# Forty of 256 tokens leave the dense expert products of a two-layer trunk, their experts' rows gathered by index

## The chip, the cores and the metric

One core of one Trainium2 chip. The metric is the device time of one execution in microseconds (us). Before the change the median of three runs is 1989.61 us (1987.29 to 1992.58). A difference of less than about 0.3% can't be told from none.

## What is computed

A trunk of two layers on T = 256 tokens of D = 1024. Layer 0 mixes tokens by a short convolution and forgetting attention, layer 1 by sparse attention (compressed, selected and window branches). After its mixer each layer has a PEER channel mixer: 8 heads choose 16 of 16384 experts of a single neuron each, by product keys (128 x 128), and sum them with softmax gates.

```python
h = modulate(rms_norm(x, norm_g), shift, scale)
q = (h @ w_q)                       # 8 heads, two halves of 64
s1, s2 = q1 @ keys1.T, q2 @ keys2.T # 128 scores each
# top 16 of each half, top 16 of the 16 x 16 sums, softmax over those 16
act = gelu(sum_d u[idx, d] * h[d])  # per token, head and chosen expert
out = sum(gate * act * v[idx])      # over 8 x 16 experts
x = x + gate_ada * out
```

Shifts, scales and gates (6 x 1024 values a layer) come from `silu(c) @ ada_w`. All is float32.

## The kernel before, in words

**Dense PEER.** The kernel doesn't look experts up. `peer(l, early, late, after)` (L689) multiplies all tokens by all 16384 rows of u, applies gelu, multiplies by a matrix that holds the gate where an expert was chosen and zero elsewhere, and multiplies by all rows of v. The 128 x 128 experts are 128 tiles of 128; the result of the u product stands in two buffers `S` of 64 tiles x 256 tokens.

**Split weights.** Every weight tile of 512 KB is loaded on SP's queue into one of five `raw` buffers (L76) and split into two parts: `hi` by an ACT copy (L82) and `lo` by a DVE subtraction (L83), three buffers each. A product of 1024 terms is then 8 slices x 3 fp32r matmuls (hi·hi, hi·lo, lo·hi; L100), each of 128 x 128 weights by 256 token columns into PSUM.

**Stages of a PEER layer.** `norm` makes h in 8 chunks of 128 features; `score` (one for each of four pairs of heads) projects with w_q and multiplies by the keys; `choose` finds the top 16 on DVE with MAX, MATCH_REPLACE and MAX_INDEX, cut into pieces that the loop below calls one by one; `weigh` makes the gates and brings them and the indices to the layout of the experts (PE transposes). `mm1(j)` is the u product of tiles j and j+1: 48 matmuls, then gelu. The first 32 calls run beside the pieces of `choose`; the second 32 each with two calls of `gating`. `gating(j)` makes, for four tokens, two one-hot matrices (L855, `is_equal`), multiplies one by the gates' high and low halves (L859, on DVE, result `w`), and contracts them by eight f16 matmuls into `pG`, which DVE multiplies into the S tiles that exist (L869) and ACT copies into those that don't yet (L871). `mm2(j)` is the v product: it splits two tiles of S (L885 on ACT, L886 on DVE) and accumulates 48 matmuls in four PSUM banks `yb`. 64 calls in all; then the residual.

**Other work in between.** `ada` (L147 to L150) loads 512 KB and reduces it on DVE (L149). The 48 of layer 1 and 8 of layer 0 are spread over peer(0): 20 in the first half of the u product, the rest in the v product. `exps` (L110) preloads the table with Ln and Exp on ACT; it stands between the u and the v product.

**What sets the order.** The tile scheduler orders instructions on each engine by its own simulation of the program, except where `keep_in_program_order` pins one. An engine takes its instructions strictly in that order.

Of the kernel before, what the change touches and what calls it, by code (L numbers as in the profile page):

```python
# [31 lines left out]
GSCALE = 2.0 ** 15  # L32

# [18 lines left out]
def trunk(ctx: ExitStack, tc: tile.TileContext, xT, c, ada_w, ada_b, norm_g, even_w, even_wf, even_bf,  # L52
          even_cw, qk_g, even_wo, odd_w, odd_wg, odd_bg, odd_g, cmp_pos, cmp_w1, cmp_w2, odd_wo,
          rel_table, buckets, w_q, keys, peer_u, peer_v, out):
# [80 lines left out]
    V.tensor_scalar(rowm, ident[:, 0:1], -31.0, None, op0=ALU.is_le)  # L135
    V.tensor_scalar(ident, ident, 0.0, None, op0=ALU.is_equal)
# [3 lines left out]
    G.iota(lane, pattern=[[1, P]], base=0, channel_multiplier=0, allow_small_or_imprecise_dtypes=True)  # L140
    mean_d = cp.tile([P, 1], F32, name="mean_d")
# [376 lines left out]
    def odd_mixer(l, w1, pos, tn, og, wg, bg, w2, mean_h):  # L518
        with tc.tile_pool(name="odd", bufs=1, reuse_waits="tile") as mp:
# [161 lines left out]
            attend(0, 3)  # L681
            for j in range(4):
                out_proj(l, odd_wo, cat, 0, j, sq)
                attend(1, j)
            for n in range(4):
                out_proj(l, odd_wo, cat, 1, n, sq)


    def peer(l, early, late, after=None):  # L689
# [3 lines left out]
        S = [s0.tile([P, 64, T], F32, name="S0"), pp.tile([P, 64, T], F32, name="S1")]  # L693
        if True:
            h = norm(l, 1, hi, lo, S[0][:, :KC], S[1][:, :KC],
                     [pp.tile([P, T], F32, tag=f"g{n}", bufs=2, name=f"h_t{n}") for n in range(2)], PEER)

# [27 lines left out]
            def parts():  # L725

                if hot[0] is None:
                    hot[0] = cp.tile([P, 4, 1024], F16, tag="x", name="hot")
                x = hot[0]
                return ([x[:, n, :512].rearrange("p (t i) -> p t i", t=4) for n in range(2)],  # L730
                        [x[:, n, 512:].rearrange("p (t j) -> p t j", t=4) for n in range(2)],
                        [x[:, 2 + n // 2, 512 * (n % 2):512 * (n % 2) + 512].rearrange("p (t u) -> p t u", u=2)
                         for n in range(4)])
# [28 lines left out]
            def choose(hp):  # L762
# [27 lines left out]
                for n in range(2):  # L790
# [9 lines left out]
                    yield  # L800

            def weigh():
# [6 lines left out]
                V.tensor_tensor(g, g, z[:, :, :, None].to_broadcast([P, 2, 8, 16]), op=ALU.mult)  # L809
                it, jt, g_hi, g_lo = parts()[2]  # L810
# [6 lines left out]
                gr = pp.tile([P, T], F32, tag="g1", bufs=2, name="gr")  # L817
                V.tensor_scalar(gr, pT[:, :T], GSCALE, None, op0=ALU.mult)
                V.tensor_copy(g_hi, gr[:, :, None].to_broadcast([P, T, 2]))
                V.tensor_tensor(g_lo, gr[:, :, None].to_broadcast([P, T, 2]), g_hi, op=ALU.subtract)  # L820
# [4 lines left out]
            def mm1(j):  # L825
# [3 lines left out]
                for s in range(2):  # L829
                    contract(p[:, s * T:(s + 1) * T], over_d(weights(peer_u[l, j + s]), h))  # L830
                p = p.rearrange("p (a t) -> p a t", a=2)
                s = S[j // 64][:, j % 64:j % 64 + 2]
                n = gated[0]
                if n < T:
# [5 lines left out]
            def gating(j):  # L840
# [3 lines left out]
                sl = slice(4 * b, 4 * b + 4)  # L844
# [6 lines left out]
                def words(v):  # L851
                    return v[:, sl, None].to_broadcast([P, 4, 64, 2])
# [23 lines left out]
            def mm2(j):  # L876
# [3 lines left out]
                vx = []  # L880
                for n in range(2):
                    s = S[j // 64][:, j % 64 + n]
                    v = weights(peer_v[l, j + n])
                    x = Op(None, h.hi[:, (j + n) % KC], h.lo[:, (j + n) % KC])
                    A.activation(x.hi, s, AF.Copy)  # L885
                    V.tensor_tensor(x.lo, s, x.hi.bitcast(F32), op=ALU.subtract)  # L886
                    vx.append((v, x))
                order = [(n, k) for n in range(2) for k in range(KC)]
                for n, k in order if j < 126 else sorted(order, key=lambda o: o[1]):
                    v, x = vx[n]  # L890
                    contract(yb[k // 2][:, (k % 2) * T:(k % 2 + 1) * T],
# [12 lines left out]
            side = pieces()  # L904
# [9 lines left out]
            start = 24  # L914
            lots = spread(early[:20], (64 - start) // 2)
            for j in range(0, 64, 2):
# [3 lines left out]
                if j >= start:  # L920
                    for f in lots[(j - start) // 2]:
                        f()
            for _ in side:
                pass
            for b in range(32):
                for _ in range(2):
                    gating(64 + 2 * b)
                mm1(64 + 2 * b)
            exps()
            for b, fs in enumerate(spread(early[20:], 32)):  # L930
                mm2(2 * b)
                for f in fs:
                    f()
            s0.release()
            got = None
            for b, fs in enumerate(spread(late, 32)):
                mm2(64 + 2 * b)
                if b == 4:
                    cur[0] = x_tile()
                    nc.sync.dma_start(cur[0], xd)  # L940
                if b == 8 and after is not None:
                    got = after()
                for f in fs:
                    f()
            for k in range(KC):
# [3 lines left out]
                else:  # L949
                    power(k, S[1][:, k])  # L950
# [9 lines left out]
    def finish(l):  # L960
        ada_done(l, 0, 6)
        gain(l, 0)
        gain(l, 1)
# [6 lines left out]
    def after():  # L970
# [3 lines left out]
    got = peer(0, adas(0, 5 * KC, 6 * KC) + [gate2] + adas(1, 0, 30),  # L974
               adas(1, 30, 6 * KC) + [lambda: finish(1)], after)
    odd_mixer(1, *got)
    oc[0].release()
    peer(1, [], [])
# [6 lines left out]
def _arrays(i):  # L985
# [52 lines left out]
    a["peer_u"] = i["peer_u"].reshape(L, P, P, KC, P).transpose(0, 2, 4, 3, 1).reshape(L, P, P, D)  # L1038
    a["peer_v"] = i["peer_v"].reshape(L, P, P, D).transpose(0, 2, 1, 3)
# [35 lines left out]
```

## Time and profile before

| | |
|---|---|
| median of the runs | 1989.61 us |
| the profiled execution's own time | 1991.12 us |
| its span in the profile | 1989.3 us |
| mean granted TensorE clock | 0.986 of full |
| PE, DVE, ACT busy | 97%, 74%, 47% of the span |
| bytes read from HBM | 369.16 MB |

The profile is of one execution, taken on the chip. PE is TensorE's matmul, PEld its weight load, DVE VectorE, ACT ScalarE, POOL GpSimd, SP SyncE (its queue issues the loads). A row of a group has line, engine, operation, out<-in with shapes and the count, then the busy time and the mean length of one in ns, then the engine's idle time just before these and what ended it. Matmuls overlap one another, so the length of one record is more than the distance from start to start.

### The profile page before, as it was taken

Reading aid. Unit: us, or ns where it says so; the run is one execution under the profiler, and the core shown is the slowest. Engines: PE = TensorE matmul, PEld = TensorE weight load, DVE = VectorE, ACT = ScalarE, POOL = GpSimd, SP = SyncE. Lnnn points to the kernel's source line nnn. Section 1 sums busy time; section 2 is a strip of 40 time slices with the busy share of each in tenths; the row PEclk is TensorE's granted clock in tenths of the full one; section 3 lists DMA queues with packets and bytes.
Section 4 is the critical chain, followed back from the end, with each engine's and each line's share of the span. In section 5 each row is a group of like instructions: output and inputs, shape, how many; then the busy total and the mean of one; then the engine's idle time right before and its main releaser. Section 6 shows DMA issues by size and latency. Waiting matters only on the chain.

```text
span 1989.3 us, 39878 instructions
## 1 busy us (share of the span) xinstructions
PE 1930.3 (97%) x15994; PEld 1859.0 (93%) x15994; DVE 1468.0 (74%) x3424; ACT 939.3 (47%) x1547; POOL 3.6 (0%) x13
## 2 busy tenths in 40 slices
PE   4899999999999999999999989999999999999999
PEld 3788999999999999999987679999999999999999
DVE  7676999789997666666656859975899975555554
ACT  3445444444444444444456654454444444444443
POOL 0000000000000000000000000000000000000000
PEclk8999999999999999999999999999999999999999
DMA  8866567855455777877743135555554555555554
GB/s 309 262 215 193 177 202 258 273 162 159 150 159 191 233 236 249 294 244 238 228 129 99 41 115 165 177 187 178 159 159 156 154 176 183 181 183 186 183 181 127
DMA packets 105621, 375.44 MB, mean 189 GB/s; under 512 B 12715, under 2 KB 16860, under 8 KB 104540
## 3 DMA queue, kind: packets, MB, share of 16 engines
q1 hardware_dynamic: 104860, 372.38, 58.0%
q8 instruction: 125, 2.05, 0.4%
q10 hardware_dynamic: 576, 0.52, 0.1%
q14 instruction: 60, 0.49, 0.1%
HBM read 369.16 MB, written 6.31 MB: 189 GB/s over the span
## 4 chain that ended last, share of the span: by engine, by line
PE 53%; issue 41%; DMA 3%; DVE 2%; ACT 1%; DVEq 0%; POOL 0%; POOLq 0%; ACTq 0%; SPq 0%
PE pmm L100 19%; PE y L100 19%; PE po L100 2%; DMA raw<-in_ada_w_dram 2%; PE pG L100 1%; PE pq L100 1%; PE pcc L100 1%; PE pwq L100 1%; PE s L638 1%; PE pv L100 1%; DMA S<-in_keys_dram 1%; PE pt L342 1%; PE po_att L653 1%; DMA raw<-in_even_w_dram 1%; PE pb L100 1%
## 5 line engine op out<-in xcount | busy, mean ns | idle before, releaser
L82 ACT ACTIVATE hi<-raw 128x1024 fp32r<-128x1024 f32 x588 | 622.1, 1059 | 899.2 <-PE pmm L100 416.3
L83 DVE TENSOR_TENSOR lo<-raw,hi 128x1024 fp32r<-128x1024 f32 x588 | 717.5, 1221 | 332.2 <-ACT hi L82 331.0
L100 PE MATMUL y<-h_hi,hi 128*128 128x256 f32 x2048 | 579.7, 284 | 6.6 <-ACT h_hi L885 6.6
L100 PE MATMUL pmm<-h_hi,hi 128*128 128x256 f32 x2048 | 584.6, 286 | 0.0
L100 PE MATMUL pmm<-h_hi,lo 128*128 128x256 f32 x2048 | 581.9, 285 | 0.7 <-DVE lo L83 0.7
L100 PE MATMUL pmm<-h_lo,hi 128*128 128x256 f32 x2048 | 582.1, 284 | 0.0
L100 PE MATMUL y<-h_lo,hi 128*128 128x256 f32 x2048 | 580.7, 284 | 0.0
L100 PE MATMUL y<-h_hi,lo 128*128 128x256 f32 x2048 | 578.9, 284 | 0.0
L100 PEld LDWEIGHTS y<-h_hi,hi 128*128 128x128 f32 x2048 | 394.4, 193 | 7.0 <-ACT h_hi L885 7.0
L100 PEld LDWEIGHTS y<-h_lo,hi 128*128 128x128 f32 x2048 | 395.2, 193 | 0.0
L100 PEld LDWEIGHTS y<-h_hi,lo 128*128 128x128 f32 x2048 | 394.0, 193 | 0.0
L100 PEld LDWEIGHTS pmm<-h_hi,lo 128*128 128x128 f32 x2048 | 391.8, 192 | 1.4 <-DVE lo L83 0.9
L100 PEld LDWEIGHTS pmm<-h_lo,hi 128*128 128x128 f32 x2048 | 392.5, 192 | 0.5
L100 PEld LDWEIGHTS pmm<-h_hi,hi 128*128 128x128 f32 x2048 | 392.5, 192 | 0.0
L149 DVE CUSTOM_DVE_ANT_0 raw<-raw,silu 128x1024 f32<-128x1024 f32 x96 | 117.2, 1223 | 93.3 <-DMA raw<-in_ada_w_dram 93.0
L859 DVE TENSOR_TENSOR w<-hot 128x512 f16<-128x512 f16 x256 | 102.8, 418 | 12.4 <-PE pG L100 12.2
L886 DVE TENSOR_TENSOR h_lo<-S,h_hi 128x256 fp32r<-128x256 f32 x256 | 106.0, 418 | 3.2 <-ACT h_hi L885 3.2
L855 DVE TENSOR_TENSOR hot<-hot,lane 128x512 f16<-128x512 f16 x256 | 104.9, 417 | 0.0
L885 ACT ACTIVATE h_hi<-S 128x256 fp32r<-128x256 f32 x256 | 101.6, 402 | 5.5 <-PE y L100 5.5
L100 PE MATMUL pG<-w,hot 128*128 128x128 f16 x1024 | 84.6, 221 | 0.0
L869 DVE TENSOR_TENSOR S<-S,pG 128x256 f32<-128x256 f32 (+5 forms) x252 | 80.1, 347 | 5.0 <-PE pG L100 4.9
L100 PEld LDWEIGHTS <-hot 128*128 128x128 f16 x1024 | 59.2, 98 | 6.8
(269 smaller groups left out, 1845.3 us busy)
## 6 DMA issues: line engine op xcount, KB each, us to landing
raw<-in_peer_u_dram SPq DMA_DIRECT2D x256, 512.0 KB, 3.6
raw<-in_peer_v_dram SPq DMA_DIRECT2D x256, 512.0 KB, 4.2
raw<-in_ada_w_dram SPq DMA_DIRECT2D x96, 512.0 KB, 4.5
raw<-in_even_w_dram SPq DMA_DIRECT2D x24, 512.0 KB, 4.6
raw<-in_odd_w_dram SPq DMA_DIRECT2D x20, 512.0 KB, 4.3
raw<-in_w_q_dram SPq DMA_DIRECT2D x16, 512.0 KB, 4.2
raw<-in_even_wo_dram SPq DMA_DIRECT2D x8, 512.0 KB, 3.5
raw<-in_odd_wo_dram SPq DMA_DIRECT2D x8, 512.0 KB, 3.5
```

The lines of the kernel that those rows point to most:

```text
L82: A.activation(hi, raw, AF.Copy)
L83: V.tensor_tensor(lo, raw, hi.bitcast(F32), op=ALU.subtract)
L100: PE.matmul(dst, a, b, start=start and n == 0, stop=stop and n == len(pairs) - 1, **kw)
L149: V.tensor_tensor_reduce(out=w, in0=w, in1=silu, op0=ALU.mult, op1=ALU.add, scale=1.0, scalar=0.0, accum_out=mods[:, l, m:m + 1])
L342: PE.transpose(pt[:, n * P:(n + 1) * P], p[:, n * P:(n + 1) * P], ident)
L638: PE.matmul(s[half][:, x:x + n + pad], qT[r, ch, t * P:(t + 1) * P], k[r, gp, :n + pad], start=True, stop=True)
L653: PE.matmul(po[r, :T], vt[:, 0, cs[half]], pt[half][:, :T], start=(b == 0), stop=False)
L855: V.tensor_tensor(pairs(x), words(v), pairs(lane[:, None].to_broadcast([P, 4, P])), op=ALU.is_equal)
L859: V.tensor_tensor(pairs(x), pairs(o), words(g), op=ALU.mult)
L869: V.tensor_tensor(s[:, :n], s[:, :n], p[:, 64 * f:64 * f + n], op=ALU.mult)
L885: A.activation(x.hi, s, AF.Copy)
L886: V.tensor_tensor(x.lo, s, x.hi.bitcast(F32), op=ALU.subtract)
```

## The change

Forty tokens (columns 0 to 39; `NS = 40`) leave the dense products. All matmuls of the u and the v product then have 216 columns instead of 256 (`TD`), and there are 54 gatings a layer instead of 64.

- `by_token` copies h of the forty tokens three times side by side (120 columns), transposes it with eight fp32 matmuls into two PSUM banks `pht` and copies it to `ht`: 120 partitions, each with one token's 1024 features. It stands ahead of `score(0)`.
- `indices` and `gates3` make the experts' numbers and gates for the forty tokens, 44 columns on 120 partitions: 128 experts a token are dealt to three partitions. Two of the three thirds are moved to their partitions by DMAs from ACT's queue.
- `dots` and `values`: 44 indirect DMAs on POOL's queue each fetch 120 rows of 4 KB of u (a second copy of it, laid out by row, is a new input), and 44 reductions on DVE multiply them by `ht`; then gelu, times the gates; then 44 more fetch rows of v, and 44 operations on DVE sum them. They use three `gat` buffers. `folded` adds the three thirds of a token into `yb` with eight fp32 matmuls near the end of the v product.
- The multiplication of the one-hot matrix by the gates goes from DVE (one operation for four tokens) to ACT (one for each token, the gate as scale).
- `mm2` splits both tiles of S with one operation on each engine.
- `exps` is called at the end of `dots`.
- Of layer 1's 48 adas 16 stay in peer(0), 24 go to the odd mixer (`meanwhile`: one with each weight tile), 8 to peer(1).

```diff
+NS = 40
+TD = T - NS
+NP = 3 * NS
+NU = 44
...
+            later = [lambda m=m: ada(l, m) for m in range(2 * KC, 5 * KC)]
+            def ahead():
+                if later:
+                    later.pop(0)()
+            meanwhile[0] = ahead
...
-        S = [s0.tile([P, 64, T], F32, name="S0"), pp.tile([P, 64, T], F32, name="S1")]
+        S = [s0.tile([P, 64, TD], F32, name="S0"), pp.tile([P, 64, TD], F32, name="S1")]
...
+            hd = h.at(lambda a: a[:, :, NS:])
+            def by_token():
+                x = pp.tile([P, D], F32, tag="gat", bufs=3, name="gat")[:, :KC * NP].rearrange("p (k g t) -> p k g t", k=KC, g=3)
+                V.tensor_copy(x, h.raw[:, :, None, :NS].to_broadcast([P, KC, 3, NS]))
+                for n in range(2):
+                    p = bank("a", "pht")
+                    for k in range(4):
+                        PE.matmul(p[:NP, k * P:(k + 1) * P], x[:, 4 * n + k].rearrange("p g t -> p (g t)"), ident,
+                                  start=True, stop=True)
+                    A.activation(ht[:NP, n * 512:(n + 1) * 512], p[:NP], AF.Copy)
...
+            def thirds(dst, src, n, w):
+                V.tensor_copy(dst[:NS, n:n + w], src(0))
+                for g in (1, 2):
+                    A.dma_start(dst[g * NS:(g + 1) * NS, n:n + w], src(g))
...
+            def gather(table, u):
+                x = pp.tile([P, D], F32, tag="gat", bufs=3, name="gat")
+                G.indirect_dma_start(out=x[:NP], out_offset=None, in_=table,
+                                     in_offset=bass.IndirectOffsetOnAxis(ap=idx[:NP, u:u + 1], axis=0))
+                return x
+            def dots():
+                got = {}
+                for u in range(NU + 2):
+                    if u < NU:
+                        got[u] = gather(peer_un, u)
+                    if u >= 2:
+                        x = got.pop(u - 2)
+                        V.tensor_tensor_reduce(out=x[:NP], in0=x[:NP], in1=ht[:NP], op0=ALU.mult, op1=ALU.add, scale=1.0,
+                                               scalar=0.0, accum_out=dot[:NP, u - 2:u - 1])
+                    yield
+                A.activation(wt[:NP], dot[:NP], AF.Gelu_apprx_tanh)
+                V.tensor_tensor(wt[:NP], wt[:NP], ga[:NP], op=ALU.mult)
+                exps()
...
+                        x, c = got.pop(u - 2)[:NP], wt[:NP, u - 2:u - 1]
...
+                            V.scalar_tensor_tensor(acc[:NP], x, c, acc[:NP], op0=ALU.mult, op1=ALU.add)
...
-                    contract(p[:, s * T:(s + 1) * T], over_d(weights(peer_u[l, j + s]), h))
+                    contract(p[:, s * TD:(s + 1) * TD], over_d(weights(peer_u[l, j + s]), hd))
...
-                    V.tensor_tensor(pairs(x), pairs(o), words(g), op=ALU.mult)
+                    for t in range(4):
+                        A.activation(x[:, t], o[:, t], AF.Copy, scale=g[:, st][:, t:t + 1])
...
-            side = pieces()
+            side, near, far = pieces(), dots(), values()
+            by_token()
             score(0)
...
-            exps()
-            for b, fs in enumerate(spread(early[20:], 32)):
+            steps = [near] * 27 + [far] * 47
+            turns = spread(steps, 60)
```

Three places show what this does to the order of the instructions. DVE in the first half of layer 0's u product, before (L740 to L786 are `choose`, L83 the split):

```order
L741 MATCH_REPLACE S_1602<-S_1602,psc_1862 128x128
L743 MAX_INDEX S_1602<-S_1602,psc_1862 128x8
L740 MAX S_1602<-psc_1862 128x8
L783 TENSOR_SCALAR S_1602<-S_1602 128x64
L784 TENSOR_SCALAR S_1602<-S_1602 128x64
L83 TENSOR_TENSOR lo<-raw,hi 128x1024
```

The same place now (L780 is the reduction of `dots`, L87 the split):

```order
L780 ISA gat,dot<-gat,ht 120x1024
L780 ISA dot 120x1
L855 MAX_INDEX S_1609<-S_1609 128x8
L852 MATCH_REPLACE S_1609<-S_1609,psc_1893 128x128
L854 MAX_INDEX S_1609<-S_1609,psc_1893 128x8
L851 MAX S_1609<-psc_1893 128x8
L780 ISA gat,dot<-gat,ht 120x1024
L780 ISA dot 120x1
L87 TENSOR_TENSOR lo<-raw,hi 128x1024
```

In the program 18 steps of `dots` are called in the second half of the u product and the rest in the v product; in the order 33 of layer 0's 44 reductions stand ahead of the first one-hot, between the pieces of `choose` and the splits, and so do 34 of layer 1's. All 44 operations of `values` stand beside the gatings.

ACT among the gatings of layer 0, before (L835 and L837 are gelu, L82 the split):

```order
L871 ACTIVATE S_1602<-pG 128x62x4 x2
L82 ACTIVATE hi<-raw 128x1024
L835 ACTIVATE S_1602<-pmm_4465 128x2x240
L837 ACTIVATE pmm_4465<-pmm_4465 128x2x16
L871 ACTIVATE S_1602<-pG 128x60x4
```

And now (L974 is the gate multiply, L783 the gelu of `dots`, L114 the preload of `exps`, L986 the copy from `pG`):

```order
L986 ACTIVATE S_1609<-pG 128x60x4
L949 ACTIVATE S_1609<-pmm_4584 128x2x196
L86 ACTIVATE hi<-raw 128x1024
L783 ACTIVATE wt<-dot 120x44
L114 ACT_TABLE_LOAD
L986 ACTIVATE S_1609<-pG 128x60x4
L86 ACTIVATE hi<-raw 128x1024
L951 ACT_TABLE_LOAD
L951 ACTIVATE pmm_4584<-pmm_4584 128x2x20
L974 ACTIVATE w_4762<-hot 128x128 x4
L974 ACTIVATE w_4767<-hot 128x128 x4
```

Eight activations of 128x128 are added for each gating. The preload of Ln and Exp stands among the gelus, which load their own table again behind it.

ACT at the norm ahead of the odd mixer, before (L177 is Ln, L178 Exp, on the power `pm` of the chunk sums):

```order
L170 ACTIVATE S_1602<-x_sb 128x256 x3
L177 ACTIVATE h_t_11838<-pm,eps 128x256
L178 ACTIVATE h_t_11838<-h_t_11838 128x256
L207 ACTIVATE h_hi<-h_sq,mods,gs 128x256 x2
L193 ACTIVATE h_raw<-h_raw,mods,gs 128x256 x2
```

And now (L188 is Ln, L189 Exp):

```order
L181 ACTIVATE S_1609<-x_sb 128x256 x4
L188 ACT_TABLE_LOAD
L188 ACTIVATE h_t_12096<-pm,eps 128x256
L189 ACT_TABLE_LOAD
L189 ACTIVATE h_t_12096<-h_t_12096 128x256
L218 ACTIVATE h_hi<-h_sq,mods,gs 128x256 x2
```

Each Ln and each Exp in the odd mixer and the norm behind it has a table load of its own ahead of it; there are 30 table loads in the program, 11 before.

## Rows read from the trace of the kernel before

**Rows 1.** The page: span, and busy time of each engine.

```profile
span 1989.3 us, 39878 instructions
PE 1930.3 (97%) x15994; PEld 1859.0 (93%) x15994; DVE 1468.0 (74%) x3424; ACT 939.3 (47%) x1547; POOL 3.6 (0%) x13
```

**Rows 2.** Windows: length, PE, PEld, DVE, ACT, POOL busy, granted clock, DMA share, GB/s.

```profile
210.00:400.00 190.00, 189.30 (x1568) 188.08 (x1568) 173.32 (x545) 86.84 (x100) 0.00 (x0) 1.00 0.71 229
400.00:616.00 216.00, 216.00 (x2031) 212.76 (x2030) 200.84 (x467) 99.52 (x189) 0.00 (x0) 1.00 0.50 158
646.00:985.00 339.00, 339.00 (x2828) 339.00 (x2827) 221.89 (x314) 159.97 (x232) 0.00 (x0) 1.00 0.75 247
1000.00:1200.00 200.00, 190.45 (x1388) 153.76 (x1388) 131.97 (x480) 114.34 (x274) 1.51 (x5) 0.98 0.32 99
1202.00:1390.00 188.00, 188.00 (x1559) 186.98 (x1558) 153.18 (x507) 86.59 (x99) 0.00 (x0) 1.00 0.56 180
1390.00:1607.00 217.00, 217.00 (x2038) 213.76 (x2037) 200.55 (x465) 99.52 (x189) 0.00 (x0) 1.00 0.50 156
1636.00:1960.00 324.00, 324.00 (x2702) 324.00 (x2701) 175.27 (x226) 153.65 (x225) 0.00 (x0) 1.00 0.58 183
```

**Rows 3.** Timeline of PE, second u half: start, length, operation.

```profile
1500.00 0.28 PE L100 MATMUL pmm<-h_lo,hi 128*128 128x256 f32 x1
1500.12 0.28 PE L100 MATMUL pmm<-h_hi,lo 128*128 128x256 f32 x1
...
1502.04 0.68 PE L100 MATMUL pG<-w,hot 128*128 128x128 f16 x9
```

**Rows 4.** Timeline of PE, odd mixer: matmuls of 512 columns.

```profile
1057.21 0.39 PE L100 MATMUL pv<-lo,h_hi 128*128 128x512 f32 x1
1057.44 0.40 PE L100 MATMUL pv<-hi,h_lo 128*128 128x512 f32 x1
```

**Rows 5.** Weight loads: the group of the v product; a timeline row of plain fp32.

```profile
L100 PEld LDWEIGHTS y<-h_hi,hi 128*128 128x128 f32 x2048 | 394.4, 193 | 7.0 <-ACT h_hi L885 7.0
...
61.90 1.20 PEld L296 LDWEIGHTS pf<-wf,h_raw 128*128 128x128 f32 x10
```

**Rows 6.** Groups of instructions on DVE: busy us, mean ns, idle before.

```profile
L83 DVE TENSOR_TENSOR lo<-raw,hi 128x1024 fp32r<-128x1024 f32 x588 | 717.5, 1221 | 332.2 <-ACT hi L82 331.0
L149 DVE CUSTOM_DVE_ANT_0 raw<-raw,silu 128x1024 f32<-128x1024 f32 x96 | 117.2, 1223 | 93.3 <-DMA raw<-in_ada_w_dram 93.0
L859 DVE TENSOR_TENSOR w<-hot 128x512 f16<-128x512 f16 x256 | 102.8, 418 | 12.4 <-PE pG L100 12.2
```

**Rows 7.** Timeline of DVE in a gating of layer 0.

```profile
501.04 0.42 DVE L859 TENSOR_TENSOR w<-hot 128x512 f16<-128x512 f16 x1
501.37 0.59 DVE L869 TENSOR_TENSOR S<-S,pG 128x256 f32<-128x256 f32 x2
```

**Rows 8.** Groups of instructions on ACT.

```profile
L337 ACT ACTIVATE p<-p,sums 128x128 f32<-128x128 f32 x8 | 2.7, 390 | 0.2 <-DVE sums L444 0.2
L110 ACT ACT_TABLE_LOAD x3 | 3.8, 1283 | 0.1
```

**Rows 9.** Timeline of ACT in a gating of layer 0.

```profile
501.81 1.06 ACT L82 ACTIVATE hi<-raw 128x1024 fp32r<-128x1024 f32 x1 [2.22 <-PE pmm L100]
502.77 0.46 ACT L871 ACTIVATE S<-pG 128x144 f32<-128x144 f32 x2
```

**Rows 10.** Timeline of PE at the head of layer 0's PEER.

```profile
183.14 0.58 PE L100 MATMUL pwq<-h_hi,hi 128*128 128x256 f32 x1 [3.61 <-ACT h_hi L207]
...
189.10 0.38 PE L100 MATMUL pwq<-h_hi,hi 128*128 128x256 f32 x1
```

**Rows 11.** DMA issues: operation and count, KB each, us to landing.

```profile
raw<-in_peer_u_dram SPq DMA_DIRECT2D x256, 512.0 KB, 3.6
X<-Xt ACTq DMA_DIRECT2D x2, 128.0 KB, 4.1
```

**Rows 12.** Timeline of PE at the same norm: plain fp32 matmuls.

```profile
177.29 1.02 PE L171 MATMUL pm<-h_sq,mean_d 128*128 128x256 f32 x4
```

More of the change, by code (lines that the diff above doesn't have):

```diff
@@ L684, in odd_mixer @@
                 attend(1, j)
+            meanwhile[0] = None
+            for f in later:
+                f()
+            ada_done(l, 3, 5)
+            gain(l, 1)
             for n in range(4):
@@ new lines, in peer, with values @@
+            sums = [None]
+            def values():
+                got = {}
+                acc = sums[0] = pp.tile([P, D], F32, tag="long", name="acc")
+                for u in range(NU + 2):
+                    if u < NU:
+                        got[u] = gather(peer_v.rearrange("l j i d -> (l j i) d"), u)
+                    if u >= 2:
+                        x, c = got.pop(u - 2)[:NP], wt[:NP, u - 2:u - 1]
+                        if u == 2:
+                            V.tensor_scalar(acc[:NP], x, c, None, op0=ALU.mult)
+                        else:
+                            V.scalar_tensor_tensor(acc[:NP], x, c, acc[:NP], op0=ALU.mult, op1=ALU.add)
+                    yield
@@ L698, in peer, with folded @@
+            def folded():
+                for k in range(KC):
+                    PE.matmul(yb[k // 2][:, (k % 2) * T:(k % 2) * T + NS], sums[0][:NP, k * P:(k + 1) * P], fold[:NP],
+                              start=False, stop=False, skip_group_check=True)
             spare = S[1][:, 32:].rearrange("p a t -> p (a t)")
@@ L919, in peer @@
                     next(side, None)
-                if j >= start:
-                    for f in lots[(j - start) // 2]:
-                        f()
             for _ in side:
                 pass
-            for b in range(32):
-                for _ in range(2):
+            for b, n in enumerate(spread(range(TD // 4), 32)):
+                for _ in n:
                     gating(64 + 2 * b)
                 mm1(64 + 2 * b)
-            exps()
-            for b, fs in enumerate(spread(early[20:], 32)):
+                if b >= 12:
+                    next(near, None)
+            steps = [near] * 27 + [far] * 47
+            turns = spread(steps, 60)
+            lots = spread(early, 28) + [[]] * 4 + spread(late, 32)
+            got = None
+            for b in range(64):
                 mm2(2 * b)
-                for f in fs:
+                for f in lots[b]:
                     f()
[L934 to L938, printed above, removed]
+                for f in turns[b] if b < 60 else ():
+                    next(f, None)
+                if b == 31:
+                    s0.release()
+                if b == 36:
                     cur[0] = x_tile()
                     nc.sync.dma_start(cur[0], xd)
-                if b == 8 and after is not None:
+                if b == 40 and after is not None:
                     got = after()
-                for f in fs:
-                    f()
+                if b == 61:
+                    folded()
             for k in range(KC):
```

89 lines of the change are left out of this document (58 added, 31 removed).

## The prediction

> **What bounds the kernel now.** I read the page first: PE is busy 97% of 1989.3 us, DVE 74%, ACT 47%, and POOL has 13 instructions in all [rows 1]. That is an average over stages with different limits, so I cut the run into stages [rows 2]: first half of the u product (210 to 400 and 1202 to 1390), second half with the gatings (400 to 616 and 1390 to 1607), v product (646 to 985 and 1636 to 1960), odd mixer (1000 to 1200). The reader is to see that PE is full in each PEER stage at a granted clock of 1.00, but that DVE stands at 173 of 190 and 201 of 216 us in the two u halves, at only 222 of 339 in the v product, and that ACT stands near half throughout. So PE sets the time, with little room on DVE in the u halves and much in the v product. The pace of PE itself: two neighbouring fp32r matmuls of 256 columns start 0.12 us apart [rows 3], and the v product of layer 1 gives the same, 324 us / 2702 = 119.9 ns [rows 2].
>
> **What a matmul of 216 columns costs.** The change narrows 12288 of them (2 layers x 2 products x 3072). Two things can set 0.120. If columns do: 512 columns start 0.23 apart [rows 4], so a column costs (230 - 120) / 256 = 0.43 ns and 40 fewer give 120 - 17 = 102.5 ns. If the weight load does: ten plain fp32 loads feeding 8-column matmuls take 1.20 us, and one fp32r load is recorded as 0.193 long [rows 5], so loads follow each other every (1.20 - 0.19) / 9 = 0.112 us even with hardly a column behind them. The fp32r load handles the same 128 columns of 4 bytes and has the same recorded length, so I take **112 ns**: a gain of 8 ns. The ends are 102.5 (load hidden) and 120 (the load already sets the pace).
>
> **The v product.** PE bounds it and DVE and ACT have room [rows 2]: -3072 x 8 = -24.6 us a layer, **-49**. The ends: 0 and 3072 x 2 x 17.5 = -107. The split of S as one operation per pair only shortens idle engines; the reductions moved in and out of it sit on DVE, which has 117 us to spare. The eight folding matmuls are under 3 us and count as nothing. DMA: u and v moved 247 GB/s at a share of 0.75 in 646 to 985 without holding PE [rows 2], which is the level that the first u half reaches when gathers join it.
>
> **First u half.** PE falls to 1536 x 0.112 = 172 us, but the scheduler has put the dots here: 33 in layer 0 and 34 in layer 1 stand before the first one-hot of the gatings, between the pieces of the choice, and DVE is taken in order. A dot is an ada's reduction with 120 for 128 rows, 1.22 us [rows 6]. Layer 0: 173.3 - 20 adas x 1.22 + 33 x 1.22 + 3 for the small index operations = 192.2. Layer 1: 153.2 + 34 x 1.22 + 3 = 197.7. DVE becomes the bound. PE's work before was 1536 x 0.120 = 184.3 in 190 us, so a stage runs 3% over its bound; I charge DVE the same: 198 and 204, that is **+8 and +16**. The gain of PE in this stage is gone.
>
> **Second u half.** ACT takes over the gate multiply. Before, one DVE operation 128x512 of 0.42 us [rows 6], whose neighbours overlap by 0.08 [rows 7], so 0.336; now four activations 128x128 with a scale per partition. The nearest row has that shape and that scale and takes 0.390 [rows 8]; neighbours on ACT overlap by 0.095 (1.06 long, the next after 0.96) [rows 9], so 0.295 each. 54 gatings x 8 x 0.295 = 127.4 us. ACT: 99.5 + 127.4 - 5 (narrower gelus and copies) + two table loads of 1.283 [rows 8] = 224.5 of a stage of 216. DVE: 200.8 - 128 x 0.336 - a sixth of the one-hots and S products (about 13) + 11 dots + 44 values x 1.2 (the split's 1.221 [rows 6] less the overlap, plus a scalar read) = 211. PE: 172 + 432 x 0.0565 [rows 3] = 196. So **ACT** bounds, where it was half idle. Before, PE had 184.3 + 512 x 0.0565 = 213 in 216, 1.3% over; ACT at 227.5 gives **+12 and +11**. The bounds: 0.195 for an activation (nothing but PE's time, gain 20) and 0.39 without overlap (+53).
>
> **Head of PEER.** The eight transposes (16 PE instructions) of by_token stand between the norm's last matmul and the first matmul of the projection. They need every chunk of h. Before, the projection's first 24 matmuls trickled from 183.14 to 189.10 behind the chunks [rows 10] and then ran at 0.12. Now PE waits until the last chunk (189), the copy and the transposes: about 193. What was done by then, 24 + 3.9 / 0.12 = 56 matmuls, is late: 56 x 0.12 = 7 us a layer, **+14**. The ends are 0 and 10 a layer.
>
> **Odd mixer.** The preload of the Ln/Exp table now follows the Gelu of the dots, in the middle of the gatings, where the next gelu loads its own table again; so the mixer and the norm after it load tables 18 times more, 18 x 1.283 = 23 us of ACT, and 22 adas x 1.22 = 27 us of DVE come into a stage of 200 us where ACT has 114 and DVE 132 [rows 2]. Hidden wholly it costs the two Exp loads directly on the chain of the norm, 3 us; wholly exposed 50. PE idles there only 10 of 200 us, so most is covered: **+12**.
>
> **Waits for gathers.** Each of eight pairs of heads now has index work and two DMAs on ACT's queue (a 128 KB one there lands in 4.1 us [rows 11]) before its first gather, and a dot whose rows are late holds the splits queued behind it on DVE, for which PE waits. With three buffers I take 1 us for each: **+8**.
>
> Sum: -49 + 8 + 16 + 12 + 11 + 14 + 12 + 8 = +32. The profiled execution took 1991.1 us, 1.5 above the median of the runs; the forecast is 1991.1 + 32 - 1.5 = **2022**.
>
> **Rivals.** (A) Columns set the pace: 102.5 ns. The u halves stay with DVE and ACT, the v products give -107 for -49: 1964. For it: 128 columns of f16 at 0.0565 [rows 3] and 512 at 0.23 lie near a line through 256. Against it: the 0.112 of bare loads. The Trainium skill (TensorE: Matmul & The Clock Gate, Back-to-back issue gap) has a column rule: an isolated matmul is N / 2.4 + 2.5 ns, which gives 92.5 for 216, and all 12288 at 27.5 less would be -338, or -169 with the v products alone; by that rule 256 columns would take 109, and the trace has 120. Chance 0.18. (B) The covers hold: no slip over the bounds (+2, +10, +8.5, +7.5), 3 for the mixer, 6 for the heads, nothing for gathers: -49 + 37 = -12, 1978. Chance 0.18. (C), slower: gathers bound. All 88 of a layer lie in the two u halves, 426 us by my sum, so from 4.8 us each they set the time; a dot waits for its rows with the splits behind it. At 5.3 us it is 40 us a layer, 2102; at 6 us 102 a layer, 2226. For it: 120 rows of 4 KB, three buffers, indices late; POOL did nothing of this before. Against it: a load of 512 KB lands in 3.6 us [rows 11]. The Trainium skill (DMA: Bandwidth & Descriptors, Anatomy of one DMA) puts a transfer issued by GpSimd at 2 us plus bytes / 436 GB/s, an estimate of 3.1 us for 480 KB; no run here shows a gather. Chance 0.14. (D) fp32r under 256 columns runs at the pace of plain fp32: four of 256 columns take 1.02 us, 0.16 of it the drain of the last (0.28 - 0.12), so 0.215 [rows 3, 12], 0.18 for 216: +12288 x 0.06 = 737, some 2760. Nothing in the trace has fp32r at such a width. Chance 0.05. That the columns are not narrowed is excluded: the order has 128x216 in both products.
>
> **How the numbers follow.** My sum 0.45, A 0.18, B 0.18, C 0.14, D 0.05. A measurement tells 0.3%, 6 us, from no change. A and half of B are faster, and a little of the sum's own spread: 0.28. The rest of B and the sum's lower edge are the same: 0.11. Slower 0.61. The range goes from 1950 (A with good covers) to 2095 (the open ends of the mixer, of ACT's activations or of slow gathers); it leaves out D, most of C and the far end of A. The sum's own range is 1990 to 2060.
>
> **What would show it.** Right: neighbouring 216-column matmuls in the v product 0.112 apart and that stage near 315 and 300 us; DVE at 95% or more in the first u half, with PE's waits there on lo; ACT at 95% or more with the gatings, w ended by ACT; some 30 table loads; the first projection matmul 10 us later after the norm. Wrong: a pitch of 0.103 or 0.120; dots that wait for gat (C); ACT's activations far from 0.295; a mixer that is not longer.

## The result, and the profile after

The changed kernel takes **2172.51 us** (median of four runs, 2162.43 to 2178.16), 1.0912 times the kernel before (95% interval 1.0868 to 1.0955). The forecast was 2022 in a range of 1950 to 2095: slower as forecast, by 182 us where 32 were forecast.

Page of the changed kernel: span, engines, and DMA queues with packets, MB and the share of 16 engines' span that they took. They answer to [rows 1].

```profile
span 2171.6 us, 40798 instructions
PE 1927.1 (89%) x15898; PEld 1838.6 (85%) x15898; DVE 1549.7 (71%) x3280; ACT 1174.2 (54%) x2289; POOL 244.5 (11%) x189
...
q1 hardware_dynamic: 104860, 372.38, 55.3%
q0 software_dynamic: 25344, 86.52, 16.1%
```

PE has lost 8 points of its share, and no other engine is near full. A new queue, q0, holds the gathers: 86.52 MB beside 372.38 MB of weights.

The windows of the changed kernel by stage, columns as in [rows 2]: first and second u half of layer 0, v product, odd mixer, then the same u halves and v product of layer 1.

```profile
218.00:456.00 238.00, 196.94 (x1600) 192.33 (x1600) 190.34 (x573) 86.25 (x103) 47.96 (x37) 0.92 0.80 218
456.00:717.00 261.00, 220.08 (x1942) 215.14 (x1941) 213.35 (x372) 217.65 (x613) 71.78 (x52) 0.91 0.85 226
718.00:1068.00 350.00, 346.61 (x3088) 345.35 (x3088) 218.39 (x254) 164.11 (x193) 0.00 (x0) 1.00 0.74 243
1083.00:1283.00 200.00, 180.32 (x1165) 138.96 (x1163) 132.18 (x453) 118.20 (x267) 1.31 (x4) 0.93 0.38 122
1326.00:1559.00 233.00, 196.64 (x1598) 192.69 (x1597) 189.59 (x572) 85.93 (x102) 48.00 (x37) 0.91 0.81 223
1559.00:1817.00 258.00, 220.43 (x1937) 216.72 (x1937) 211.86 (x368) 217.05 (x613) 73.07 (x52) 0.90 0.90 229
1820.00:2167.00 347.00, 346.87 (x3088) 346.54 (x3088) 198.71 (x215) 161.17 (x189) 0.00 (x0) 1.00 0.63 201
```

In the u halves PE is busy 197 of 238 and 220 of 261 us, at a granted clock of 0.90 to 0.92 instead of 1.00. DVE has 80 to 82% of the stage and ACT 83 to 84% of the second half: neither fills it. The v products are full again, and shorter.

Where the time went, stage by stage, in PE's timeline (us). A head runs from the norm's last power matmul to the first u matmul, a u product to the first v matmul, a v product to its last matmul. The expectations below count a u product to its own last matmul, up to 4 less.

| stage | before | after | difference | forecast |
|---|---|---|---|---|
| head of PEER, both layers | 32.6, 31.6 | 38.8, 42.5 | +17 | +14 |
| u product, both layers | 412.1, 411.2 | 500.1, 493.9 | **+171** | +47, +8 for gathers |
| v product, both layers | 371.3, 370.3 | 349.6, 347.0 | -45 | -49 |
| last v matmul to last power matmul (odd mixer) | 176.6 | 215.8 | **+39** | +12 |

With half a microsecond at the end this is the whole 182. Two terms hold the error: the u product and the mixer.

The v product is what was forecast. Timeline of PE in the v product of layer 1, to set against [rows 3]:

```profile
2000.04 0.27 PE L104 MATMUL y<-h_lo,hi 128*128 128x216 f32 x1
2000.15 0.27 PE L104 MATMUL y<-h_hi,lo 128*128 128x216 f32 x1
2000.26 0.28 PE L104 MATMUL y<-h_hi,hi 128*128 128x216 f32 x1
```

Starts 0.11 us apart: the pace of the bare weight loads, which [rows 5] put at 0.112, and not the 0.1025 of the columns.

Now a piece of the first u half, some 25 us after the first gather. Timeline of ACT and DVE (L86 is the `hi` copy that a split needs, L780 a dot, L87 the split), and of PE at the same time:

```profile
280.21 1.06 ACT L86 ACTIVATE hi<-raw 128x1024 fp32r<-128x1024 f32 x1 [1.85 <-PE pmm L104]
280.24 1.20 DVE L87 TENSOR_TENSOR lo<-raw,hi 128x1024 fp32r<-128x1024 f32 x1
282.98 1.23 DVE L780 CUSTOM_DVE_ANT_0 gat<-gat,ht 120x1024 f32<-120x1024 f32 x1 [1.53 <-DMA gat<-in_peer_un_dram,idx]
284.13 0.08 DVE L780 DVE_READ_ACCUMULATOR2_ANT dot<- 120x1 f32 x1
284.13 1.22 DVE L87 TENSOR_TENSOR lo<-raw,hi 128x1024 fp32r<-128x1024 f32 x1
```

```profile
284.38 0.28 PE L104 MATMUL pmm<-h_lo,hi 128*128 128x216 f32 x1
285.40 0.37 PE L104 MATMUL pmm<-h_hi,lo 128*128 128x216 f32 x1 [0.74 <-DVE lo L87]
```

DVE stands 1.53 us for the rows of a dot, although the split behind it could run (its `hi` was ready at 281.27); PE comes to that split's `lo` and stands too. The waits of the changed kernel's first u half (218 to 456: engine, line, what it waited for, us in total, times, longest) add such pieces up:

```profile
DVE gat L780 <- DMA gat<-in_peer_un_dram,idx: 44.8, 18, 6.3
...
PE pmm L104 <- DVE lo L87: 36.5, 18, 6.0
```

And the window of the first eleven gathers, 262 to 293:

```profile
262.00:293.00 31.00, 21.08 (x164) 20.36 (x162) 23.82 (x64) 9.12 (x12) 10.48 (x9) 0.89 0.95 239
```

PE is busy 21 of 31 us, DVE 24, and the DMA engines are at 0.95 of their time while they move 239 GB/s. By queue in that window (packets, MB, share), and the queue of the rows over the whole of a run described below, which fetches half of each row:

```profile
q0 software_dynamic: 1286, 4.40, 56.5%
q1 hardware_dynamic: 819, 2.99, 38.4%
...
q0 software_dynamic: 14080, 43.27, 6.8%
```

In the window a byte of either queue takes the same DMA time: 4.40 MB in 56.5% and 2.99 MB in 38.4% of 31 us are 251 GB/s each. The half rows moved 43.27 MB in 6.8% of 2084.0 us, 305 GB/s. A row is thus hardly dearer than a weight tile; both slow down when they are moved side by side through nearly full engines.

### The profile page after: what moved, and what is told of

It is laid out like the page before. It is cut to its first block, busy times and chain, and to the rows that moved or that the text cites. A ratio compares the mean times of both kernels' runs of the same rounds, so it can differ in the third digit from the quotient of the medians.

```text
span 2171.6 us, 40798 instructions
## 1 busy us (share of the span) xinstructions
PE 1927.1 (89%) x15898; PEld 1838.6 (85%) x15898; DVE 1549.7 (71%) x3280; ACT 1174.2 (54%) x2289; POOL 244.5 (11%) x189
## 3 DMA queue, kind: packets, MB, share of 16 engines
q1 hardware_dynamic: 104860, 372.38, 55.3%
q0 software_dynamic: 25344, 86.52, 16.1%
## 4 chain that ended last, share of the span: by engine, by line
PE 50%; DMA 23%; DVE 14%; issue 7%; ACT 4%; POOL 2%; DVEq 0%; POOLq 0%; ACTq 0%
PE y L104 31%; DMA gat<-in_peer_v_dram,idx 10%; DMA gat<-in_peer_un_dram,idx 9%; PE pmm L104 6%; DVE lo L87 5%; DMA raw<-in_ada_w_dram 3%; PE po L104 2%; POOL gat L768 2%; DVE acc L801 1%; ACT w L974 1%; PE pcc L104 1%; ACT hi L86 1%; PE pwq L104 1%; DVE S L855 1%; DVE S L852 1%
## 5 line engine op out<-in xcount | busy, mean ns | idle before, releaser
L86 ACT ACTIVATE hi<-raw 128x1024 fp32r<-128x1024 f32 x588 | 621.8, 1059 | 812.3 <-PE y L104 354.1
L87 DVE TENSOR_TENSOR lo<-raw,hi 128x1024 fp32r<-128x1024 f32 x588 | 713.9, 1220 | 275.0 <-ACT hi L86 274.1
L104 PE MATMUL pmm<-h_hi,lo 128*128 128x216 f32 x2048 | 596.1, 292 | 78.0 <-DVE lo L87 78.0
L104 PE MATMUL pmm<-h_hi,hi 128*128 128x216 f32 x2048 | 597.1, 292 | 56.9 <-DVE S L952 53.8
L104 PE MATMUL pmm<-h_lo,hi 128*128 128x216 f32 x2048 | 592.2, 290 | 0.0
L104 PE MATMUL y<-h_hi,lo 128*128 128x216 f32 x2048 | 562.1, 275 | 2.3 <-DVE lo L87 2.3
L104 PE MATMUL y<-h_hi,hi 128*128 128x216 f32 x2048 | 561.5, 275 | 2.6 <-ACT h_hi L998 2.6
L104 PE MATMUL y<-h_lo,hi 128*128 128x216 f32 x2048 | 562.6, 275 | 0.7 <-DVE h_lo L999 0.6
L974 ACT ACTIVATE w<-hot 128x128 f16<-128x128 f16 x864 | 263.5, 393 | 30.6 <-DVE hot L933 14.3
L768 POOL DMA_INDIRECT gat<-in_peer_un_dram,idx x88 | 117.9, 1340 | 854.0 <-DVE S L853 281.2
L780 DVE CUSTOM_DVE_ANT_0 gat<-gat,ht 120x1024 f32<-120x1024 f32 x88 | 107.3, 1221 | 99.3 <-DMA gat<-in_peer_un_dram,idx 99.3
L768 POOL DMA_INDIRECT gat<-in_peer_v_dram,idx x88 | 122.9, 1397 | 225.4 <-DVE acc L801 177.8
L801 DVE SCALAR_TENSOR_TENSOR acc<-gat,wt,acc 120x1024 f32<-120x1024 f32 x86 | 110.1, 1280 | 49.0 <-DMA gat<-in_peer_v_dram,idx 48.1
```

The lines of the kernel that those rows point to most:

```text
L86: A.activation(hi, raw, AF.Copy)
L87: V.tensor_tensor(lo, raw, hi.bitcast(F32), op=ALU.subtract)
L104: PE.matmul(dst, a, b, start=start and n == 0, stop=stop and n == len(pairs) - 1, **kw)
L768: G.indirect_dma_start(out=x[:NP], out_offset=None, in_=table, in_offset=bass.IndirectOffsetOnAxis(ap=idx[:NP, u:u + 1], axis=0))
L780: V.tensor_tensor_reduce(out=x[:NP], in0=x[:NP], in1=ht[:NP], op0=ALU.mult, op1=ALU.add, scale=1.0, scalar=0.0, accum_out=dot[:NP, u - 2:u ...
L801: V.scalar_tensor_tensor(acc[:NP], x, c, acc[:NP], op0=ALU.mult, op1=ALU.add)
```

## The experiments

Theory A: the bytes. While gathers run, they and the weights want more of the DMA engines than there is; rows come late, DVE waits in order, PE behind it. Theory B: the gather as such, an indexed fetch of scattered rows with three in flight, however many bytes. Theory C: DVE and ACT themselves, as the forecast had it, only larger. The seven experiments on the changed kernel are one run each; its own four runs lie 16 us apart, so a difference of a few us tells nothing.

**No rows at all.**

```diff
-                G.indirect_dma_start(out=x[:NP], out_offset=None, in_=table,
-                                     in_offset=bass.IndirectOffsetOnAxis(ap=idx[:NP, u:u + 1], axis=0))
+                G.tensor_copy(x[:NP, 0:1], idx[:NP, u:u + 1])
```

> Leaves out all 176 gathers: POOL copies the index into one column of a fixed buffer instead, so dots and values keep their place, their waits for indices and their DVE time, but move no rows. Theories A and B: the u products fall to the bounds of DVE and ACT that were forecast, near 430 us each, total 2030 to 2050. Theory C: they stay above 480, total 2150 or more.

Measured: 2064.34 us; u products 439.5 and 441.7 us. Windows of this run, layer 0's u halves:

```profile
220.00:430.00 210.00, 195.97 (x1674) 192.72 (x1673) 203.16 (x595) 91.95 (x109) 32.05 (x46) 0.97 0.54 171
431.00:657.00 226.00, 203.87 (x1870) 200.32 (x1870) 196.93 (x349) 209.79 (x604) 21.83 (x42) 0.92 0.44 139
```

Now DVE is at 203 of 210 us in the first half, and ACT at 210 of 226 in the second: the two bounds of the forecast. The second half is as long as forecast (226 for 228), the first 12 us longer (210 for 198). C explains 27 and 30 us; the rows cost the other 61 and 52. C alone falls.

**Half of each row.**

```diff
-                G.indirect_dma_start(out=x[:NP], out_offset=None, in_=table,
+                G.indirect_dma_start(out=x[:NP, :D // 2], out_offset=None, in_=table.rearrange("r (a d) -> (r a) d", a=2),
```

> Leaves out half of each fetched row: the same 88 gathers a layer of 120 pieces, each of 2 KB instead of 4, and the DVE operations read that half twice, as many elements as before. The u product of the changed kernel took 499 and 492 us (409 and 408 before). Theory A (the DMA engines are full: u weights and gathers together need more than they move, about 245 GB/s): the bytes of a u product fall from 110 to 89 MB, and it ends near 430 us, where DVE and ACT set the pace; total 2040 to 2070. Theory B (the time of a gather from issue to landing, three in flight, and DVE's splits queued behind a dot that waits; bytes matter little): the u products stay within 20 us, total 2140 or more. Theory C (DVE and ACT themselves): no change, 2165 or more.

Measured: 2085.81 us; u products 452.7 and 455.1. As many gathers, half the bytes: 47 and 39 of the 61 and 52 us come back, three quarters of them. B as it stood falls. A's 430 was not reached either, and could not be, with the bounds at 440; the total is 16 us over A's range. The DMA engines were not full any more: 0.67 and 0.61 of the halves of layer 0's u product, for 0.80 and 0.85.

**The same bytes without looking up.**

```diff
-                G.indirect_dma_start(out=x[:NP], out_offset=None, in_=table,
-                                     in_offset=bass.IndirectOffsetOnAxis(ap=idx[:NP, u:u + 1], axis=0))
+                G.tensor_copy(x[:NP, 0:1], idx[:NP, u:u + 1])
+                G.dma_start(x[:NP], table[128 * (l * P + u):128 * (l * P + u) + NP])
```

> Leaves out the looking up: each gather becomes a plain DMA from POOL's queue of 120 rows that lie one behind the other (the same 480 KB, the same buffers), behind a POOL copy of the index so that it waits for what the gather waited for. If the bytes are what fills the DMA engines (theory A): the u products stay within 20 us of the changed kernel's 499 and 492. If it is the fetching of scattered rows by an index (theory B): they fall to 440 to 455, near the 437 and 440 of the run that moves no rows.

Measured: 2158.64 us; u products 491.5 and 493.0, less than 9 us from the changed kernel's. That the rows are scattered and found by an index costs little or nothing; that 480 KB of them are wanted does. From issue to landing such a transfer took 8.1 us (count, KB, median us):

```profile
gat<-in_peer_un_dram POOLq DMA_DIRECT2D x88, 480.0 KB, 8.1
```

**Half rows, six buffers.** To the run with half rows:

```diff
-                x = pp.tile([P, D], F32, tag="gat", bufs=3, name="gat")
+                x = pp.tile([P, D // 2], F32, tag="gat", bufs=6, name="gat")
...
-                    if u >= 2:
+                    if u >= LEAD:
```

with `LEAD = 5`.

> Leaves out the same half of each row as the run with half rows, and uses the space so won for six row buffers of 2 KB instead of three of 4: five gathers are in flight ahead of the dot that reads the oldest. With three buffers the u products took 452 and 455 us, with no rows moved 437 and 440. If what is left between these is the landing time of rows that are asked for too late: 437 to 443 now. If it is the bytes: 450 or more.

Measured: 2058.88 us; u products 439.1 and 445.9, against 452.7 and 455.1 with three buffers and 439.5 and 441.7 without rows. All of what was left in layer 0 comes back, and two thirds in layer 1, with the same bytes: for half rows, it was rows that landed after DVE was ready, and more of them in flight hide it. For full rows, with the DMA engines at 0.80 to 0.90, this is argued and not shown: full rows with more buffers were not tried.

**Dots and values held to their place in the program.**

```diff
-                        V.tensor_tensor_reduce(out=x[:NP], in0=x[:NP], in1=ht[:NP], op0=ALU.mult, op1=ALU.add, scale=1.0,
+                        tc.keep_in_program_order(V.tensor_tensor_reduce(out=x[:NP], in0=x[:NP], in1=ht[:NP], op0=ALU.mult, op1=ALU.add, scale=1.0,
...
-                            V.scalar_tensor_tensor(acc[:NP], x, c, acc[:NP], op0=ALU.mult, op1=ALU.add)
+                            tc.keep_in_program_order(V.scalar_tensor_tensor(acc[:NP], x, c, acc[:NP], op0=ALU.mult, op1=ALU.add))
```

> The dots and the values are held behind the DVE instruction ahead of them in the program, so 18 dots run with the gatings, 26 dots and all values in the v product; the table preload moves into the v product with them, and the program has 10 table loads. Theory A: the u products fall to 420 to 440 us, and the v products grow, because 67 MB of weights and 34 MB of rows at 245 GB/s want 410 us where 350 were needed; mixer 15 us shorter; total 2080 to 2130. Theory B: as A for the u product, the v product grows by 20 us or less, total 2020 to 2050. Theory C: u products 430, v products as they are, total 2020.

Measured: 2090.57 us; u products 399.8 and 395.7, below the 420 of A, v products 416.8 and 402.7, A's 410. Windows of this run: the u halves and the v product of layer 0, and of that v product the two waits in question.

```profile
218.00:397.00 179.00, 177.41 (x1581) 175.89 (x1580) 151.18 (x506) 88.53 (x114) 5.15 (x3) 1.00 0.64 200
397.00:611.00 214.00, 204.27 (x1967) 201.09 (x1965) 169.93 (x336) 209.65 (x600) 18.99 (x16) 0.98 0.64 192
618.00:1034.00 416.00, 369.40 (x3083) 360.64 (x3083) 295.38 (x347) 163.95 (x192) 98.04 (x68) 0.96 0.99 282
```

```profile
ACT hi L86 <- DMA raw<-in_peer_v_dram: 154.3, 71, 13.2
...
PEld y L104 <- DVE lo L87: 36.8, 34, 5.2
```

The first half without dots is bounded by PE again (177 of 179 us, 12 less than before the change), the second by ACT with the gate multiply (210 of 214). The v product, with 34 MB of rows beside 67 MB of weights, has the DMA engines at 0.99, and now it is the weights that come late. The cost of the rows was not taken away, only moved.

**The table preload back between u and v.**

```diff
                 V.tensor_tensor(wt[:NP], wt[:NP], ga[:NP], op=ALU.mult)
-                exps()
...
+            exps()
             steps = [near] * 27 + [far] * 47
```

> Only the table preload goes back between the u and the v product (10 table loads for 30). The odd mixer took 205 us from the last v matmul of layer 0 to the last power matmul of layer 1, 166 before. If the table loads cost that: 15 to 25 us less. If the adas put into the mixer cost it: under 6 us less.

Measured: 2155.66 us; the mixer's stretch 208.1 for 215.8 (the 205 and 166 above end at the first of the norm's power matmuls, not the last), the head of layer 1 38.6 for 42.5. The twenty table loads that it takes out (the traces have 10 in this run and before the change, 30 in the changed kernel) cost some 12 us there, 8 of them in the mixer's stretch; they are not its 39.

**The adas back in peer(0).**

```diff
-            meanwhile[0] = ahead
...
-    got = peer(0, adas(0, 5 * KC, 6 * KC) + [gate2] + adas(1, 0, KC), adas(1, KC, 2 * KC) + [first2], after)
+    got = peer(0, adas(0, 5 * KC, 6 * KC) + [gate2] + adas(1, 0, 30), adas(1, 30, 6 * KC) + [lambda: finish(1)], after)
```

> All 48 adas of layer 1 go back to where they were before the change, in peer(0): 20 of the early ones in the first half of layer 0's u product, the rest in its v product; nothing else is undone, so the mixer keeps its extra table loads. From the last v matmul of layer 0 to the last power matmul of layer 1 the changed kernel took 216 us, 177 before; taking the table loads out gave 8 back. If the adas cost the rest (their loads ahead of the mixer's own weights on SP's queue, their reductions ahead of the splits on DVE): this stretch falls to about 185. If something else does: it stays above 205. Layer 0's first u half, already short of DMA, should get 5 to 15 us longer, its v product up to 10.

Measured: 2190.22 us; the mixer's stretch 184.2, the 185 expected. The adas cost 32 us of the 39. But layer 0's u product grew by 26 us to 526.1 and its v product by 14 to 363.6: the 17 MB of the 32 that came back cost at least about as much where they were as where they went. That moving them paid is not shown: layer 1's u product, to which no ada was added, also came out 10 us longer (504.0), more than the balance of 8.

**A version that spreads the bytes.**

```diff
-NS = 40
+NS = 28
...
-                x = pp.tile([P, D], F32, tag="gat", bufs=3, name="gat")
+                x = pp.tile([P, D], F32, tag="gat", bufs=2, name="gat")
...
-            steps = [near] * 27 + [far] * 47
+            steps = [near] * (LEAD + 1) + [far] * (NU + LEAD)
```

> A version built on the reading that bytes in flight are what hurts: 28 tokens leave the dense products instead of 40 (228 columns), their experts in four groups of 28 partitions, so 32 gathers of 112 rows where there were 44 of 120 (14.7 MB a product for 21.6); two row buffers instead of three, dots held to the gatings (one a step) and values to the v product; the gates' low half multiplied on DVE again; the transposes behind two projections instead of ahead of the first; adas as before the change but for eight in peer(1). Theory A: u products near 390 us, where PE, DVE and ACT are balanced, v products 350 to 370 if 96 MB in 350 us can be had, head and mixer as before; total 1890 to 1950. If bytes do not matter but each gather does (theory B), the v products stay near 400 and the total near 2000. It also shows the pace at 228 columns: 0.112 if the weight load sets it, 0.107 if columns do.

Measured: **1961.67 us**, 0.9841 times before (0.9801 to 0.9881). u products 393.6 and 389.3, v products 394.7 and 347.7. Layer 1 does what A says; layer 0's v product, with 28 adas beside the values, does not, and the total is 12 us over A's range. 228 columns also start 0.112 apart.

> As v1, with 16 of layer 1's adas taken from layer 0's v product (28 there in v1, 12 here) to the second part of the odd mixer, held to their place in the program: that v product moved 250 GB/s and took 395 us, while layer 1's, with 15 MB less, took 348; the mixer's second part moved 36 to 123 GB/s. If bytes set that stage it falls to about 355 and the mixer grows by 5 to 15: 1925 to 1940. If the adas' reductions on DVE are what costs, the mixer takes back what the v product gives: 1950 to 1965.

```diff
+            later = [lambda m=m: ada(l, m) for m in range(3 * KC, 5 * KC)]
...
             gates()
+            meanwhile[0] = ahead
             attend(0, 0)
```

Measured: **1928.19 us**, 0.9707 times before (0.9690 to 0.9725), the fastest that computes everything. Windows of this run, layer 0: u halves, v product, odd mixer.

```profile
216.00:400.00 184.00, 178.26 (x1560) 175.18 (x1560) 170.84 (x532) 88.03 (x109) 3.00 (x2) 1.00 0.74 241
400.00:606.00 206.00, 201.41 (x1988) 199.02 (x1986) 200.26 (x427) 158.40 (x403) 29.89 (x29) 1.00 0.75 229
610.00:960.00 350.00, 344.62 (x3070) 343.14 (x3069) 244.89 (x264) 165.64 (x195) 60.19 (x32) 1.00 0.85 265
968.00:1145.00 177.00, 168.78 (x1180) 132.23 (x1179) 127.90 (x448) 99.57 (x253) 1.51 (x5) 0.99 0.41 130
```

PE is busy 95 to 98% of every stage at a clock of 0.99 to 1.00. The DMA engines stand at 0.74 to 0.85 in the products. The changed kernel's u halves averaged 0.80 to 0.90, with bursts at 0.95. Sixteen adas in the mixer's second part, where DMA and DVE had room, cost 5 us there (183.4 for 178.2) and gave 42 in the v product.

**The same without the 28 tokens.** All their work is left out of v2; zeros are folded in.

> As v2, with all work for the 28 tokens left out: no transposes of h for them, no indices, gathers, dots or values; zeros are folded in. What v2 pays for them is the difference. By the stage times of v2 (u products 391 and 387, v products 353 and 348, where PE's own need is 372 and 344) it is 20 to 40 us: 1890 to 1910. If more bytes still hurt v2, more: 1880 or less.

Measured: 1890.57 us, 0.9512 times before (0.9478 to 0.9545). So v2 still pays 38 us for the 28 tokens, and the narrower matmuls with the other edits are worth 99.

## Why the prediction was wrong

**Right.** The pitch: 112 ns was taken between 102.5 and 120, and 111 to 112 was measured at 216 and 228 columns; the v products gave 45 us for 49. The bounds of DVE and ACT: with no rows the u products took 439.5 and 441.7 where the sum has 198 + 228 and 204 + 228, 426 and 432; that is 58 us over before, for the 47 of the sum. A gate multiply on ACT was put at 0.295 us; thirteen of them take 3.90 in the changed kernel:

```profile
599.66 3.90 ACT L974 ACTIVATE w<-hot 128x128 f16<-128x128 f16 x13
```

The head: the transposes stand where the order put them, and the first projection matmul starts at 192.47 for 183.14 [rows 10]:

```profile
189.05 3.71 PE L733 MATMUL pht<-ident,gat 128*120 128x128 f32 x16 [9.63 <-DVE gat L729]
192.47 0.41 PE L104 MATMUL pwq<-h_hi,hi 128*128 128x256 f32 x1
```

Of the +17 of both heads 4 were layer 1's table loads. Behind two projections, in v1 and v2, both heads took 35 to 36 us, +7: about half of the other 13 went with the place, though 28 tokens instead of 40 may have a part in it.

**Wrong, and most of the error: "Waits for gathers", +8, and the sentence on DMA under the v product.** It compared two rates, 247 GB/s seen and about that wanted, and concluded that the rows fit. Three things were missed.

First, the sum by stage: the order puts all 88 gathers of a layer beside the u product, 43 MB to 67 MB of weights, 110 MB in 426 us, 259 GB/s. That is more than the 247 it was compared with.

Second, a rate is not a share. The 247 GB/s went with a share of 0.75 in a stage where the weights were alone. The u halves of layer 0 moved 218 and 226 GB/s, less than that, and the engines stood at 0.80 and 0.85: with both queues in flight a byte takes more DMA time, 251 GB/s in the first burst against 330 (247 / 0.75) with the weights alone. 0.80 of 238 us and 0.85 of 261 us are 412 us of engine time, where the sum gave the whole u product 426: 97%, and that fits only if nothing comes in bursts. The scheduler made bursts: eleven dots as soon as a pair of heads has its indices, 33 us of gathers, then about as long without. In the first such burst the share was 0.95.

Third, rival (C) had the right place and the wrong point. It let gathers decide from 4.8 us each. The first eleven were issued like this (timeline of POOL):

```profile
257.59 2.19 POOL L768 DMA_INDIRECT gat<-in_peer_un_dram,idx  x1 [254.85 <-DVE S L852]
...
290.87 1.16 POOL L768 DMA_INDIRECT gat<-in_peer_un_dram,idx  x1 [0.92 <-DVE dot L780]
```

Ten steps in 33.3 us, 3.3 each, and all 88 of layer 0 from 257.59 to 646.69, 4.5 each: faster than the 4.8, and still they cost. A gather needn't be the bound to cost; it is enough that a dot waits on DVE with a split behind it. The sentence "a dot whose rows are late holds the splits queued behind it" stood in the prediction, with 1 us for each of eight pairs of heads; the first half of layer 0 alone has 44.8 us of such waits. The runs give the rows' cost as 113 us for both layers (994.0 less 881.1), in place of 8.

The page rule weighed there, the Trainium skill (DMA: Bandwidth & Descriptors, Anatomy of one DMA), makes a transfer of 480 KB issued by GpSimd 3.1 us by estimate. The run with plain rows has 8.1 us from issue to landing for the same bytes beside the weights, so the trace doesn't agree. The estimate is of one transfer, and as a reason against (C) it said nothing of one beside a stream of others.

**Wrong, smaller: "Odd mixer", +12.** Its ends were 3 and 50, and 39 came. The table loads, priced at up to 23, were 8 in this stretch; the 22 adas, priced as DVE time that is mostly covered, were 32. Their loads stand on SP's queue with the mixer's own weights, and their reductions on DVE ahead of what PE waits for; which of the two weighs more was not told apart. The end of layer 0 shows a part of it: before the change the residual (L236, now L247) follows the v product at once (two rows); now (the others; timeline of DVE):

```profile
992.63 2.55 DVE L236 SCALAR_TENSOR_TENSOR x_sb<-y,gq,x_sb 128x256 f32<-128x256 f32 x6 [0.69 <-PE y L100]
995.50 0.87 DVE L236 SCALAR_TENSOR_TENSOR x_sb<-y,gq,x_sb 128x256 f32<-128x256 f32 x2 [0.32 <-PE y L100]
...
1066.62 1.23 DVE L160 CUSTOM_DVE_ANT_0 raw<-raw,silu 128x1024 f32<-128x1024 f32 x1 [2.52 <-DMA raw<-in_ada_w_dram]
...
1067.78 1.22 DVE L87 TENSOR_TENSOR lo<-raw,hi 128x1024 fp32r<-128x1024 f32 x1
1068.91 2.44 DVE L247 SCALAR_TENSOR_TENSOR x_sb<-y,gq,x_sb 128x256 f32<-128x256 f32 x6
1071.46 1.23 DVE L160 CUSTOM_DVE_ANT_0 raw<-raw,silu 128x1024 f32<-128x1024 f32 x1
```

The residual's first six chunks (L247) wait behind an ada that itself waits 2.52 us for its load, and the last two behind another. From the last v matmul to the last power matmul of the next norm it is 14.8 us, 5.9 before: 9 of the 39.

**Also wrong:** what the prediction wanted to see in the u halves, DVE and ACT at 95% or more, did not come: it was 80% and 83%, and even with the rows gone 97% and 93%.

**The clock.** In the u products it averaged 0.90 to 0.92, where it was 1.00 before and 0.99 to 1.00 in v2. The trace has its two levels one by one. In the u product it first fell to 1.2 GHz at 267.7, inside a wait of PE for a split that stood behind dots. At that level the matmuls start 0.21 us apart, at 2.4 GHz 0.11 (the wait, a window at the lower level, and PE's timeline in it):

```profile
270.17 0.55 PE L104 MATMUL pmm<-h_hi,lo 128*128 128x216 f32 x1 [5.98 <-DVE lo L87]
...
295.10:305.20 10.10, 8.20 (x39) 7.94 (x38) 8.26 (x19) 2.46 (x3) 0.00 (x0) 0.50 0.81 213
...
300.13 0.41 PE L104 MATMUL pmm<-h_hi,lo 128*128 128x216 f32 x1
300.35 0.41 PE L104 MATMUL pmm<-h_hi,hi 128*128 128x216 f32 x1
```

Summed over PE's records of layer 0's u product, PE's waits of over 0.15 us are 82 us, and the matmuls at the lower level cost 31 us more than they would at 0.112; with no rows it is 39 and 17. So of the 61 us that the rows cost there, some 43 are waits and some 14 the lower clock (in layer 1 34 and 18 of 52).

**Left open:** whether more buffers would hide full rows, and how the adas' 32 us divide between their loads and their reductions.

## What to carry to other kernels

Sum the bytes by stage, in the order that the scheduler really gave, and against the rate that the DMA engines reach when both streams are in flight, not the one seen with one stream alone: a transfer that fits on average still costs when it comes in bursts. A wait for a DMA that is put on an in-order engine costs everything queued behind it, so ask how far ahead the transfer is issued and how many buffers that takes. And look where a queue is idle before moving loads: 22 adas spread over the mixer from its start cost 32 us, and in another version sixteen of them 5 us in its second part.

## What the runs showed of the hardware

The pace of fp32r matmuls with a weight load each, at the upper clock: 0.120 us at 256 columns, 0.112 at 228, 0.111 to 0.112 at 216, so the last twelve columns gained nothing; at the lower clock 0.213 at 216. Fetching 120 scattered rows of 4 KB by index costs the kernel about what a plain transfer of the same bytes from the same queue does (2172.51 and 2158.64 us), which I had not expected to be so close. Rows and weights side by side, with the DMA engines at 0.95, moved 251 GB/s of the DMA time that each took; weights alone 330 (247 GB/s at 0.75), half rows 305.
